# A sixth 8 KB gather buffer, idle tiles as further ones, and smaller scratch pools in a two-layer mixer with an expert layer

## The chip, the cores and the metric

The kernel runs on one core of a Trainium2 chip. The metric is the device time of one execution in microseconds (us). A core has five engines that each work through their own stream of instructions in order: TensorE (PE; PEld is its weight load), VectorE (DVE), ScalarE (ACT), GpSimd (POOL) and SyncE (SP). Sixteen DMA engines move data between HBM and the on-chip memory. In this kernel SP issues ordinary transfers (queue q1) and POOL issues the gathers by index (queue q0).

## What is computed

Two layers act on 256 latent tokens and 256 context tokens of width 1024, in float32. Each layer is a mixer (layer 0: a gated DeltaNet, "gdn", beside RWKV-7; layer 1: window attention beside a Hyena convolution) and behind it an expert layer, PEER. In layer 0 both streams go through both parts; in layer 1 only the latent stream does, while the attention reads the context's keys. The expert layer, cut to what matters:

```python
def peer(h, peer_wq, peer_k1, peer_k2, peer_u, peer_v):
    ...
        best, pos = lax.top_k(cand, PEER_TOPK)
        eid = jnp.take_along_axis(cid, pos, axis=-1)
        gate = jax.nn.softmax(best, axis=-1)
        u = jnp.take(peer_u, eid, axis=0)
        act = jax.nn.gelu(jnp.einsum('bthkd,btd->bthk', u, xb).astype(F32))
        vsel = jnp.take(peer_v, eid, axis=0)
        return jnp.einsum('bthk,bthkd->btd', (gate * act).astype(xb.dtype), vsel)
```

Every token has 8 heads with 16 experts each out of 16384, so 128 rows of u and 128 rows of v, each of 1024 numbers. Rows u and v of an expert lie side by side in HBM, 8 KB in all.

## The kernel before

Tokens are worked on in tiles of 128. `experts()` does one tile (or part of one): for each n of 128, POOL gathers the n-th expert's row for each of the 128 tokens (L1277) into a tile of the tag g8, 8 KB on each partition and 1 MB in all. VectorE multiplies its u half with the token and sums (L1280). ScalarE and VectorE make the gated activation from that (L1286 to L1289), ScalarE puts it on a diagonal, di (L1290), and TensorE multiplies di with the v half, 512 columns at a time, and adds into two banks of PSUM, pv (L1292). The profile shows two records for each of these two matmuls. The gathered buffer comes free when the second has read it.

There are 768 gathers: context tiles pc[0] (128) and pc[1] (64 first, 64 later, split at CUT), latent tiles pl[0] and pl[1], and in layer 1 p3[0] and p3[1]. At the end of a tile `experts()` takes a g8 tile for the residual and, in layer 1, another for the final norm. g8 also holds blocks of mod_w (1 MB each), from which `adaln` makes the modulation at the start.

Buffers: `Net.t(tag, shape)` takes a tile of a tag, and the dictionary BUFS says how many buffers a tag has (1 where it isn't named). A tile that finds none free waits until an older one's last reader is done. The tags that the change touches: g8; t2, s2 and sy, scratch tiles of the mixers (2 KB a partition for t2 and s2 at their widest); gx (one column, made in L1288) and gsum, small tiles of the expert layer and its preparation. s2 also holds the transposed probabilities PT of a pair of heads in `attention` (transposes L1524, copies L1526, matmuls L1530), while eight s2 tiles hold the output weights wo. h8 and qkT are single tiles: h8 is the layer's input in transposed form (two tiles long), and both hold query weights of PEER in layer 1 (`keep_wq`).

The order is not written out by hand. Python lays the steps down in program order, with generators that mix stages (`mix`, `some`, `rest`) and marks that hold a stage back (`issue_after`), and a scheduler simulates the program and puts each engine's instructions in the order in which they become ready there, expert steps filling in beside the mixers. The numbers of buffers enter that simulation, so they change the order on all engines. The stages in time: modulation and context mixer (0 to about 490 us), experts of the context beside the latent mixer (to about 1256), the latent tile's output projection and preparation of its experts (to about 1352), then experts beside the second layer's mixer and, to the end, alone.

The gathers' descriptors are written by POOL into a memory that `dynamic_dma_scratch_size` sizes, 4096 bytes before.

Of the kernel before, what the change touches and what calls it, by code (L numbers as in the profile page):

```python
# [20 lines left out]
D = 1024  # L21
# [7 lines left out]
def _lay(i):  # L29
# [83 lines left out]
    for n in ("b1", "b2", "freq"):  # L113
# [32 lines left out]
    return A  # L146


BUFS = dict(w=3, t2=9, t4=3, s2=10, AT=4, XT=2, N=2, sy=8, g8=5, ei=16, ef=2, best=2, pos=2, i16f=2, eid=2, pk=2, pf=2, gate=4, v16=2, i16=2, kTh=2, ftok=2,
            act=2, gz=3, gx=3, di=3, fnr=2, gsum=2, rT=2, nr=4, nr2=2, nr3=2, am=4, t2r=2, t2v=2, t2v2=2)  # L150
PBUFS = dict(gm=3, sc=3, pv=2)
CUT = 64

# [1 line left out]
class Net:  # L155
# [14 lines left out]
    def t(self, tag, shape, dt=F32):  # L170
        self.n += 1
        if tag in PBUFS:
            return self.psum[tag].tile(shape, dt, name=f"{tag}_{self.n}", tag=tag)
        return self.sb.tile(shape, dt, name=f"{tag}_{self.n}", tag=tag, bufs=BUFS.get(tag, 1))

# [1084 lines left out]
        nc.vector.reciprocal(gs, gs)  # L1260
        nc.vector.scalar_tensor_tensor(gate, gate, 0.5 / RT2PI, gs[:, :, None].to_broadcast([128, m, 16]), op0=ALU.mult, op1=ALU.mult)

    def experts(self, l, xin, cond, p, dst, fin=None, ns=range(128)):


        nc, A = self.nc, self.A
        h = p.h
        if h is None:
            h = self.t("h4", [128, D])
            nc.sync.dma_start(h, p.hd)  # L1270
        if p.act is None:
            p.act = self.t("act", [128, 128])
        act, gate = p.act, p.gate.rearrange("p h k -> p (h k)")
        pv = [self.t("pv", [128, 512]) for _ in range(2)]
        for n in ns:
            uv = self.t("g8", [128, 2 * D])
            nc.gpsimd.indirect_dma_start(out=uv, out_offset=None, in_=A[l + "peer_uv"],  # L1277
                                         in_offset=bass.IndirectOffsetOnAxis(ap=p.ei[n // 16][:, n % 16:n % 16 + 1], axis=0))
            x = act[:, n:n + 1]
            ins = nc.vector.scalar_tensor_tensor(uv[:, :D], uv[:, :D], RT2PI, h, op0=ALU.mult, op1=ALU.mult, accum_out=x)  # L1280
            if n == ns[0] + 8:
                self.mark = ins.ins
            with self.tc.high_priority():

                z, xg, di = self.t("gz", [128, 2]), self.t("gx", [128, 1]), self.t("di", [128, 128])
                nc.scalar.activation(z[:, 0:1], x, AF.Square, scale=math.sqrt(0.044715) / RT2PI)  # L1286
                nc.scalar.activation(z[:, 0:1], z[:, 0:1], AF.Tanh, scale=x, bias=x)  # L1287
                nc.vector.tensor_mul(xg, x, gate[:, n:n + 1])  # L1288
                nc.scalar.activation(z[:, 1:2], z[:, 0:1], AF.Identity, scale=xg, bias=xg)  # L1289
                nc.scalar.activation(di, self.ident, AF.Copy, scale=z[:, 1:2])  # L1290
                for hf in range(2):
                    nc.tensor.matmul(pv[hf], lhsT=di, rhs=uv[:, D + hf * 512:D + (hf + 1) * 512], start=n == ns[0], stop=n == ns[-1])  # L1292
            yield
        xr = self.t("g8", [128, 2, D])
        x1, rgt = xr[:, 0], xr[:, 1]
        nc.sync.dma_start(x1, xin)
        nc.sync.dma_start(rgt, self.mod[l][cond:cond + 1, 5 * D:6 * D].to_broadcast([128, D]))
        for hf in range(2):
            cs = slice(hf * 512, (hf + 1) * 512)
            nc.vector.tensor_mul(rgt[:, cs], pv[hf], rgt[:, cs])  # L1300
            nc.vector.tensor_add(x1[:, cs], x1[:, cs], rgt[:, cs])
        if fin:
            xf = self.t("g8", [128, 2, D])
            fn = xf[:, 0]
            nc.sync.dma_start(fn, A[fin].to_broadcast([128, D]))
            r = self.rstd(x1, "fn", xf[:, 1])
            nc.vector.scalar_tensor_tensor(x1, x1, r, fn, op0=ALU.mult, op1=ALU.mult)
        if ns[0] == 0 or "x2d1" in self.want:
            nc.sync.dma_start(dst, x1)
        self.xlast = x1  # L1310
# [350 lines left out]
    def whole(self, out):  # L1661
        nc, tc, A = self.nc, self.tc, self.A
        with ExitStack() as es:
# [5 lines left out]
            x1 = [self.d(f"x1d{c}", [T, D]) for c in range(2)]  # L1669
            x2 = [[self.d(f"x2d{c}{i}", [128, D]) for i in range(2)] for c in range(2)]  # L1670
            x3 = [self.d(f"x3d{i}", [128, D]) for i in range(2)]
            row = lambda a, i: a[i * 128:(i + 1) * 128]
            lat, ctx, odd = Stream(), Stream(), Stream()
            pc, pl, p3 = [], [], []
# [14 lines left out]
            def peer(*a, **k):  # L1689
                rest(self.experts(*a, **k))  # L1690
# [91 lines left out]
            some(g, 7)  # L1782
            peer("l0_", row(x1[1], 0), 1, pc[0], x2[1][0])
            peer("l0_", row(x1[1], 1), 1, pc[1], x2[1][1], ns=range(CUT))
            peer("l0_", row(x1[0], 0), 0, pl[0], x2[0][0])
            with tc.issue_after(self.mark):
                rest(g)
            peer("l0_", row(x1[0], 1), 0, pl[1], x2[0][1])
# [47 lines left out]
            for i in range(2):  # L1836
                self.dumprow("x3d", x3[i], i)
            self.dump("yT", odd.yT[0])
            peer("l1_", x3[1], 0, p3[1], row(out, 1), "fnorm")


class Stream:
# [19 lines left out]
```

## Time and profile before

| | |
|---|---|
| runs (us) | 3276.64, 3277.8, 3294.03; median 3277.8 |
| profiled execution (us) | 3273.96, its span 3272.2 |
| TensorE busy (us) | 2603.5 (80% of the span) |
| VectorE busy (us) | 1957.6 (60%) |
| ScalarE busy (us) | 1395.2 (43%) |
| GpSimd busy (us) | 987.4 (30%) |
| moved by DMA | 1020.52 MB, of which 805.36 by gathers |

The profile is of one execution. Busy shares are means over stages with different limits, so the table by stage below shows for each stretch how long each engine was busy and which share of the sixteen DMA engines' time was in use. A row of waits names the engine and the line that stood still, what ended the wait, and the total, the number and the longest of such waits. "<-PE pv L1292" behind a POOL instruction means that it waited for that matmul.

### The profile page before, as it was taken

What the parts mean: (1) busy time and instruction counts of PE and PEld (TensorE: products, weight loads), DVE (VectorE), ACT (ScalarE), POOL (GpSimd) and SP (SyncE); (2) the same over time, 40 slices, a digit from 0 to 9 for tenths busy, and PEclk for the clock granted to TensorE, in tenths of its full rate; (3) what the DMA queues carried; (4) which work ended last, traced back from release to release, by engine and by line L of the source; (5) the groups of instructions that cost most, each with busy time, mean ns of one, the idle gap of its engine ahead of it and who ended that gap; (6) DMA issues with size and microseconds to landing.
All of it is one profiled execution on the core that took longest, in us unless ns stands there. A gap on an engine that the chain in (4) does not pass through costs nothing.

```text
span 3272.2 us, 40186 instructions
## 1 busy us (share of the span) xinstructions
PE 2603.5 (80%) x12216; PEld 1447.9 (44%) x12216; DVE 1957.6 (60%) x5457; ACT 1395.2 (43%) x3953; POOL 987.4 (30%) x834
## 2 busy tenths in 40 slices
PE   6986867988888978696977777779967987767776
PEld 4765745754454535462422222235545543222222
DVE  2566546777956665579755555456547687554554
ACT  1431113465445545233554455544433544544554
POOL 0001202222322321124554344433202333434553
PEclk8886978999989989898999899999989999999999
DMA  9675549899889996587899999999947899999998
GB/s 324 214 230 143 191 143 343 318 343 335 322 290 333 339 319 206 214 305 260 298 379 385 355 387 384 378 371 347 363 153 284 306 338 352 377 369 379 384 390 324
DMA packets 296222, 1020.52 MB, mean 312 GB/s; under 512 B 64383, under 2 KB 167104, under 8 KB 197704
## 3 DMA queue, kind: packets, MB, share of 16 engines
q0 software_dynamic: 110592, 805.36, 64.5%
q1 hardware_dynamic: 185416, 212.60, 20.1%
q8 instruction: 99, 1.62, 0.2%
q14 instruction: 115, 0.94, 0.1%
HBM read 995.62 MB, written 22.25 MB: 311 GB/s over the span
## 4 chain that ended last, share of the span: by engine, by line
PE 32%; DMA 27%; issue 16%; DVE 14%; POOL 7%; ACT 3%; SPq 1%; POOLq 0%; DVEq 0%; ACTq 0%
DMA g<-in_l_peer_uv_dram,ei 17%; PE pv L1292 12%; POOL g L1277 6%; DVE g L1280 5%; PE gm L269 4%; PE gm L1142 3%; PE gm L1621 1%; DMA t<-in_l_mod_w_dram 1%; PE sc L269 1%; PE gm L277 1%; DMA w<-in_l_peer_wq_dram 1%; DMA qkT<-in_l_peer_wq_dram 1%; PE pv L356 1%; DMA g<-in_l_mod_w_dram 1%; DMA t<-l_mod 1%
## 5 line engine op out<-in xcount | busy, mean ns | idle before, releaser
L1292 PE MATMUL pv<-g,di 128*128 128x512 f32 x3072 | 1556.5, 635 | 421.7 <-ACT di L1290 420.4
L1277 POOL DMA_INDIRECT g<-in_l_peer_uv_dram,ei x768 | 927.6, 1208 | 1901.8 <-PE pv L1292 1109.7
L1292 PEld LDWEIGHTS pv<-g,di 128*128 128x128 f32 x3072 | 558.3, 198 | 1229.5 <-ACT di L1290 778.3
L1280 DVE SCALAR_TENSOR_TENSOR g<-g,h 128x1024 f32<-128x1024 f32 x384 | 469.8, 1224 | 309.3 <-DMA g<-in_l_peer_uv_dram,ei 304.2
L1286 ACT ACTIVATE gz<-act 128x1 f32<-128x1 f32 x768 | 154.8, 202 | 973.7 <-DVE g L1280 972.7
L1289 ACT ACTIVATE gz<-gz,gx 128x1 f32<-128x1 f32 x768 | 296.5, 386 | 68.6 <-DVE gx L1288 44.1
L1290 ACT ACTIVATE di<-c_ident,gz 128x128 f32<-128x128 f32 x768 | 307.6, 401 | 29.6 <-PE pv L1292 7.2
L1287 ACT ACTIVATE gz<-gz,act 128x1 f32<-128x1 f32 x768 | 296.2, 386 | 23.5
L1280 DVE SCALAR_TENSOR_TENSOR g<-g,vtok 128x1024 f32<-128x1024 f32 x128 | 157.0, 1227 | 155.3 <-DMA g<-in_l_peer_uv_dram,ei 153.3
L1280 DVE SCALAR_TENSOR_TENSOR g<-g,ktok 128x1024 f32<-128x1024 f32 x128 | 158.1, 1236 | 106.0 <-DMA g<-in_l_peer_uv_dram,ei 104.9
L1280 DVE SCALAR_TENSOR_TENSOR g<-g,yv 128x1024 f32<-128x1024 f32 x128 | 156.1, 1219 | 90.6 <-DMA g<-in_l_peer_uv_dram,ei 90.4
L269 PE MATMUL gm<-h,w 128*128 128x256 f32 x752 | 175.4, 380 | 2.1 <-DMA w<-in_l_w_in_dram 2.1
L269 PEld LDWEIGHTS gm<-h,w 128*128 128x128 f32 x752 | 141.3, 190 | 43.4 <-issue 24.4
L1288 DVE TENSOR_TENSOR gx<-act,gate 128x1 f32<-128x1 f32 x768 | 121.3, 158 | 52.0 <-ACT gz L1286 1.4
L1214 DVE MAX8 v<-t 128x8 f32<-128x128 f32 x64 | 15.5, 284 | 92.9 <-ACT t L1157 53.2
L1621 PE MATMUL gm<-og,w 128*128 128x128 f32 x384 | 52.4, 295 | 16.4 <-DMA w<-in_l_peer_wq_dram 16.4
L1621 PEld LDWEIGHTS gm<-og,w 128*128 128x128 f32 x384 | 51.0, 210 | 25.0 <-DMA w<-in_l_peer_wq_dram 17.0
L356 PE MATMUL pv<-t,scond 128*32 128x256 f32 x384 | 38.2, 493 | 28.8 <-DMA t<-in_l_mod_w_dram 28.7
L612 DVE TENSOR_TENSOR kTh<-dg 128x30 f32<-128x30 f32 (+14 forms) x120 | 40.2, 335 | 25.1 <-DMA dg<-dndg 22.8
L636 POOL MEMSET XT<- 32x512 f32 x4 | 2.1, 516 | 172.8 <-PE sc L269 172.7
L277 PE MATMUL gm<-w,h 128*128 128x256 f32 x192 | 47.9, 395 | 5.3 <-DMA w<-in_l_w_in_dram 5.3
L277 PEld LDWEIGHTS gm<-w,h 128*128 128x128 f32 x192 | 37.0, 197 | 17.9 <-issue 13.4
(686 smaller groups left out, 3127.9 us busy)
## 6 DMA issues: line engine op xcount, KB each, us to landing
w<-in_l_w_in_dram SPq DMA_DIRECT2D x70, 512.0 KB
g<-in_l_mod_w_dram SPq DMA_DIRECT2D x24, 1024.0 KB
t<-in_l_mod_w_dram SPq DMA_DIRECT2D x48, 512.0 KB
w<-in_l_peer_wq_dram SPq DMA_DIRECT2D x26, 512.0 KB
g<-in_l_peer_uv_dram,ei POOLq DMA_INDIRECT x768, 8.2
qkT<-in_l_peer_wq_dram SPq DMA_DIRECT2D x9, 1024.0 KB
XT<-in_l_peer_wq_dram SPq DMA_DIRECT2D x14, 512.0 KB
XT<-in_l_w_in_dram SPq DMA_DIRECT2D x10, 512.0 KB
```

The source lines that it names most:

```text
L269: self.nc.tensor.matmul(ps[:, m], lhsT=wt[q][:, k, m * 128:(m + 1) * 128], rhs=hk, start=q == 0 and m == 0 and k == 0, stop=q == 1 and m = ...
L277: self.nc.tensor.matmul(ps, lhsT=hk[:, i * 128:(i + 1) * 128], rhs=wt[k // 4][:, k % 4], start=k == 0, stop=k == KC - 1)
L1142: nc.tensor.matmul(pq[:, m], lhsT=w[1][k // 4][:, k % 4, m * 128:(m + 1) * 128], rhs=hT[i][:, k], start=k == 0, stop=k == KC - 1)
L1277: nc.gpsimd.indirect_dma_start(out=uv, out_offset=None, in_=A[l + "peer_uv"], in_offset=bass.IndirectOffsetOnAxis(ap=p.ei[n // 16][:, n % ...
L1280: ins = nc.vector.scalar_tensor_tensor(uv[:, :D], uv[:, :D], RT2PI, h, op0=ALU.mult, op1=ALU.mult, accum_out=x)
L1286: nc.scalar.activation(z[:, 0:1], x, AF.Square, scale=math.sqrt(0.044715) / RT2PI)
L1287: nc.scalar.activation(z[:, 0:1], z[:, 0:1], AF.Tanh, scale=x, bias=x)
L1288: nc.vector.tensor_mul(xg, x, gate[:, n:n + 1])
L1289: nc.scalar.activation(z[:, 1:2], z[:, 0:1], AF.Identity, scale=xg, bias=xg)
L1290: nc.scalar.activation(di, self.ident, AF.Copy, scale=z[:, 1:2])
L1292: nc.tensor.matmul(pv[hf], lhsT=di, rhs=uv[:, D + hf * 512:D + (hf + 1) * 512], start=n == ns[0], stop=n == ns[-1])
L1621: nc.tensor.matmul(pq[:, m], lhsT=wt[k // 4][:, k % 4, m * 128:(m + 1) * 128], rhs=hT[:, k], start=k == 0, stop=k == KC - 1)
```

## The change

It gives g8 six buffers instead of five, takes one buffer each from t2, s2, sy, gx and gsum, and halves the descriptor memory to 2048 bytes. `experts()` gets an argument `more`: behind each six tiles of g8 it takes one tile of each tag named there. For pl[0] that is h8 (seven buffers in a cycle), for the last tile, p3[1], h8 and qkT (eight). Both tags have one buffer and are between uses in those stretches. Line numbers behind L1276 are larger by one in the changed kernel.

```diff
-BUFS = dict(w=3, t2=9, t4=3, s2=10, AT=4, XT=2, N=2, sy=8, g8=5, ei=16, ef=2, best=2, pos=2, i16f=2, eid=2, pk=2, pf=2, gate=4, v16=2, i16=2, kTh=2, ftok=2,
-            act=2, gz=3, gx=3, di=3, fnr=2, gsum=2, rT=2, nr=4, nr2=2, nr3=2, am=4, t2r=2, t2v=2, t2v2=2)
+BUFS = dict(w=3, t2=8, t4=3, s2=9, AT=4, XT=2, N=2, sy=7, g8=6, ei=16, ef=2, best=2, pos=2, i16f=2, eid=2, pk=2, pf=2, gate=4, v16=2, i16=2, kTh=2, ftok=2,
+            act=2, gz=3, gx=2, di=3, fnr=2, gsum=1, rT=2, nr=4, nr2=2, nr3=2, am=4, t2r=2, t2v=2, t2v2=2)
...
-    def experts(self, l, xin, cond, p, dst, fin=None, ns=range(128)):
+    def experts(self, l, xin, cond, p, dst, fin=None, ns=range(128), more=()):
...
         for n in ns:
-            uv = self.t("g8", [128, 2 * D])
+            c = (n - ns[0]) % (BUFS["g8"] + len(more))
+            uv = self.t("g8" if c < BUFS["g8"] else more[c - BUFS["g8"]], [128, 2 * D])
...
-            peer("l0_", row(x1[0], 0), 0, pl[0], x2[0][0])
+            peer("l0_", row(x1[0], 0), 0, pl[0], x2[0][0], more=("h8",))
...
-            peer("l1_", x3[1], 0, p3[1], row(out, 1), "fnorm")
+            peer("l1_", x3[1], 0, p3[1], row(out, 1), "fnorm", more=("h8", "qkT"))
...
-    nc = bacc.Bacc("TRN2", target_bir_lowering=False, num_devices=1, dynamic_dma_scratch_size=4096)
+    nc = bacc.Bacc("TRN2", target_bir_lowering=False, num_devices=1, dynamic_dma_scratch_size=2048)
```

TensorE at the start of the latent gdn_scan (L684, L691, L707 are its steps, L1292 the matmuls of a context expert). Before:

```order
L684 MATMUL sc_1138_6997<-S0_67_288,qkT_912_5471 64x128 x8
L684 MATMUL sc_1139_6998<-S0_67_288,qkT_912_5471 64x128 x4
L1292 MATMUL pv_1892_10046<-g8_2094_10698,di_2097_10703 128x512
L1292 MATMUL pv_1893_10047<-g8_2094_10698,di_2097_10703 128x512
L684 MATMUL sc_1139_6998<-S0_67_288,qkT_912_5471 64x128 x4
L691 MATMUL sc_1142_7019<-s2_1140_7015,h8_1111_6737 64x64 x16
L1292 MATMUL pv_1892_10046<-g8_2098_10711,di_2101_10716 128x512
L1292 MATMUL pv_1893_10047<-g8_2098_10711,di_2101_10716 128x512
L707 MATMUL sc_1143_7046<-s2_1141_7016,s2_1137_6980 64x64 x8
L707 MATMUL sc_1144_7057<-s2_1141_7016,s2_1137_6980 64x64 x8
```

TensorE at the same place after the change:

```order
L684 MATMUL sc_1138_6997<-S0_67_288,qkT_912_5471 64x128 x8
L684 MATMUL sc_1139_6998<-S0_67_288,qkT_912_5471 64x128 x8
L691 MATMUL sc_1142_7019<-s2_1140_7015,h8_1111_6737 64x64 x16
L707 MATMUL sc_1143_7046<-s2_1141_7016,s2_1137_6980 64x64 x8
L707 MATMUL sc_1144_7057<-s2_1141_7016,s2_1137_6980 64x64 x8
```

Before, 178 gathers' matmuls stand ahead of the second L684 step and 14 of the context's 192 follow among the scan's steps; after, all 192 stand ahead of it.

POOL's gathers for the latent tile pl[0] (the seventh and its neighbours; the name in front is the tile that the gather fills). Before:

```order
L1277 DMA g8_2174_10956<-in_l0_peer_uv_dram,ei_1250_7723 128x2048
L1277 DMA g8_2178_10969<-in_l0_peer_uv_dram,ei_1250_7723 128x2048
L1277 DMA g8_2182_10982<-in_l0_peer_uv_dram,ei_1250_7723 128x2048
L1277 DMA g8_2186_10995<-in_l0_peer_uv_dram,ei_1250_7723 128x2048
L1277 DMA g8_2190_11008<-in_l0_peer_uv_dram,ei_1250_7723 128x2048
```

POOL's gathers for the same tile after the change:

```order
L1278 DMA g8_2174_10956<-in_l0_peer_uv_dram,ei_1250_7723 128x2048
L1278 DMA h8_2178_10969<-in_l0_peer_uv_dram,ei_1250_7723 128x2048
L1278 DMA g8_2182_10982<-in_l0_peer_uv_dram,ei_1250_7723 128x2048
L1278 DMA g8_2186_10995<-in_l0_peer_uv_dram,ei_1250_7723 128x2048
L1278 DMA g8_2190_11008<-in_l0_peer_uv_dram,ei_1250_7723 128x2048
```

The seventh gather of the tile, and each seventh from there on, goes into h8; the order of the gathers themselves is the same.

## Rows read from the trace of the kernel before

**Rows 1.** The page: DMA queue q0, chain by line, the gathers' group.

```profile
q0 software_dynamic: 110592, 805.36, 64.5%
...
DMA g<-in_l_peer_uv_dram,ei 17%; PE pv L1292 12%; POOL g L1277 6%; DVE g L1280 5%; PE gm L269 4%; PE gm L1142 3%; PE gm L1621 1%; DMA t<-in_l_mod_w_dram 1%; PE sc L269 1%; PE gm L277 1%; DMA w<-in_l_peer_wq_dram 1%; DMA qkT<-in_l_peer_wq_dram 1%; PE pv L356 1%; DMA g<-in_l_mod_w_dram 1%; DMA t<-l_mod 1%
...
L1277 POOL DMA_INDIRECT g<-in_l_peer_uv_dram,ei x768 | 927.6, 1208 | 1901.8 <-PE pv L1292 1109.7
```

**Rows 2.** Stretches: window, length, busy time by engine, clock, DMA share, GB/s.

```profile
490.00:1256.00 766.00, 666.70 (x3736) 404.14 (x3738) 528.66 (x1541) 393.18 (x1114) 214.38 (x202) 0.93 0.91 325
1256.00:1352.00 96.00, 62.99 (x460) 49.33 (x456) 45.85 (x155) 22.55 (x73) 0.46 (x2) 0.87 0.40 131
1352.00:1560.00 208.00, 158.22 (x706) 99.32 (x707) 162.17 (x610) 76.72 (x236) 67.09 (x52) 0.89 0.83 300
1560.00:1800.00 240.00, 194.22 (x421) 72.21 (x420) 141.55 (x292) 119.84 (x342) 120.01 (x89) 0.99 0.92 352
1800.00:2164.00 364.00, 263.57 (x538) 94.63 (x538) 185.57 (x413) 179.43 (x522) 160.23 (x128) 0.97 0.97 378
2164.00:2400.00 236.00, 212.03 (x640) 119.88 (x640) 127.60 (x283) 101.04 (x288) 63.38 (x60) 0.94 0.95 356
2400.00:2480.00 80.00, 61.24 (x384) 52.55 (x384) 43.91 (x165) 23.36 (x67) 4.69 (x5) 0.92 0.22 73
2480.00:2750.00 270.00, 224.83 (x920) 136.26 (x920) 204.75 (x699) 119.52 (x365) 78.93 (x72) 0.96 0.90 333
2750.00:3272.00 522.00, 376.36 (x734) 131.24 (x732) 267.30 (x589) 255.04 (x740) 236.87 (x179) 0.96 0.95 370
```

**Rows 3.** DMA of 1860 to 2140: GB/s in 40 slices, q0, issues to landing.

```profile
GB/s 426 373 410 397 375 399 421 342 412 344 398 386 341 424 391 364 417 351 410 400 351 377 357 425 360 413 370 386 403 348 404 312 424 399 375 380 425 323 419 373
...
q0 software_dynamic: 14792, 107.69, 98.0%
...
g<-in_l_peer_uv_dram,ei POOLq DMA_INDIRECT x102, 8.5
```

**Rows 4.** Two dips of the DMA share, columns as in Rows 2.

```profile
1464.00:1476.00 12.00, 10.46 (x52) 7.99 (x53) 4.76 (x27) 3.40 (x10) 0.94 (x1) 0.72 0.48 170
...
2684.00:2700.00 16.00, 13.51 (x50) 9.33 (x51) 8.13 (x31) 5.31 (x17) 3.67 (x3) 0.82 0.62 200
```

**Rows 5.** Waits of VectorE in 1352 to 1560: total, times, longest.

```profile
DVE g L1280 <- DMA g<-in_l_peer_uv_dram,ei: 18.8, 13, 3.7
```

**Rows 6.** The same in 1560 to 2400.

```profile
DVE g L1280 <- DMA g<-in_l_peer_uv_dram,ei: 311.8, 225, 8.4
```

**Rows 7.** The same in 2480 to 2750.

```profile
DVE g L1280 <- DMA g<-in_l_peer_uv_dram,ei: 24.6, 20, 3.1
```

**Rows 8.** The same in 490 to 1256.

```profile
DVE g L1280 <- DMA g<-in_l_peer_uv_dram,ei: 73.9, 48, 4.1
```

**Rows 9.** The stretch 1216 to 1256, columns as in Rows 2.

```profile
1216.00:1256.00 40.00, 38.37 (x474) 23.19 (x474) 27.36 (x59) 32.41 (x110) 11.84 (x11) 0.97 0.72 265
```

**Rows 10.** Groups by line in 1214 to 1256: count, busy and mean, idle before.

```profile
L1292 PE MATMUL pv<-g,di 128*128 128x512 f32 x44 | 22.8, 655 | 1.1 <-ACT di L1290 1.1
```

**Rows 11.** POOL's timeline: start, duration, instruction, idle before and its releaser.

```profile
1255.31 0.94 POOL L1277 DMA_INDIRECT g<-in_l_peer_uv_dram,ei  x1 [0.39 <-PE pv L1292]
...
1351.79 0.94 POOL L1277 DMA_INDIRECT g<-in_l_peer_uv_dram,ei  x1 [95.54 <-issue]
```

**Rows 12.** TensorE's timeline in the attention of latent tile 0.

```profile
2442.11 1.90 PE L1530 MATMUL gm<-S,s 128*128 128x64 f32 x16
```

**Rows 13.** ScalarE's timeline at the same place.

```profile
2440.20 1.07 ACT L1526 COPY s<-gm 128x512 f32<-128x512 f32 x2 [0.23 <-PE gm L1524]
```

**Rows 14.** SP's queue, loads of the context's rwkv_scan into s2 tiles.

```profile
291.08 0.32 SPq L882 DMA_DIRECT2D s<-kr  x1
294.28 0.32 SPq L883 DMA_DIRECT2D s<-bk  x1
```

**Rows 15.** TensorE's timeline, the first reader of these loads.

```profile
301.91 1.95 PE L892 MATMUL pv<-s,s 64*128 64x128 f32 x16
```

## The prediction

> **What bounds the kernel now.** I read the page first. TensorE is busy for four fifths of the span, which looks like a bound; but the queue of the gathers, q0, took 64.5% of the sixteen DMA engines' time for 805.36 MB, and the chain of waits gives gathers landing (17%) more of the span than the expert matmuls (12%) [rows 1]. The 768 gathers of L1277 waited 1109.7 us for "PE pv L1292", that is for a free g8 buffer, whose last reader is that matmul [rows 1].
>
> The table by stage then tells which resource is short where [rows 2]. From 490 us on the DMA engines are busy for 0.83 to 0.97 of each stretch that holds gathers, and for 0.40 and 0.22 of the two that hold nearly none. In 1860 to 2140, a stretch of gathers only, q0 alone moved 107.69 MB at 98.0% [rows 3]. One gather is 8192 bytes times 128 rows and 144 packets (110592 / 768), so its 14792 packets are 102.7 gathers in 280 us at that load, and 0.98 x 280 / 102.7 = **2.67 us of DMA for one gather**. No buffer gets a gather under that; the actual pitch there was 280 / 102.7 = 2.73. A sixth buffer can win only time in which the DMA engines stood idle.
>
> **Term 1: idle DMA that another buffer fills, from 1352 us on.** The idle share times the length of the stretches of [rows 2] from 1352 on, without 2400 to 2480, is 35 + 19 + 11 + 12 + 27 + 26 = 130 us. It comes in dips: a mixer step holds an in-order engine, the buffers in flight land, and no free one is left for the next issue. The DMA shares in slices of 4 us give 30 such dips; two of the larger ones stand in [rows 4]. An added buffer puts one more gather into a dip, so a dip pays back at most its idle time and at most 2.67 us for each added buffer: one in most tiles, two in pl[0] (1352 to about 1750), three in the last tile (about 2896 to 3256). So the dip of [rows 4] at 2684, with 16 x 0.38 = 6.1 us idle, pays 2.67, and the one at 1464, with 12 x 0.52 = 6.2, pays 5.3. Summed so by stretch of [rows 2]: 29.0, 12.9, 4.3, 8.3, 15.6 and 3.8 us. It also pays only if VectorE later stood waiting for a gather. That wait is 18.8 us in 1352 to 1560, 311.8 in 1560 to 2400 and 24.6 in 2480 to 2750 [rows 5 to 7]; it cuts only the first figure, to 18.8. The upper bound is 18.8 + 12.9 + 4.3 + 8.3 + 15.6 + 3.8 = 64 us. The lower is 0: the buffer after a long mixer step is freed by the same matmul, and expert n+6 may be held by the same TensorE, VectorE or ScalarE queue as n+5. I take the middle, **-32**, since no row prefers an end.
>
> **Term 2: the context experts in 490 to 1256.** Two things move. VectorE waited 73.9 us there for gathers [rows 8], and the DMA was idle for 0.09 x 766 = 69 us [rows 2], so the sixth buffer may help as above. And the order of TensorE changes: before, the latent gdn_scan (L684 and after) runs between the last 14 experts, which are all done ahead of it after the change (the fences on the change). In 1216 to 1256 TensorE was busy for 38.37 of 40 us, the DMA for 0.72 of it [rows 9], and the experts' matmuls were 22.8 us of it [rows 10]. So the scan alone would be some 23 us shorter, and 14 x 2.67 = 37 us of gathers must fit into the work ahead. If all of that fits into idle DMA, the stretch wins 23 and what the waits give besides, up to 60 in all; if nothing fits, it loses 37 - 23 = 14. Ahead of 1216 the idle DMA is 69 - 40 x 0.28 = 58 us, more than 37, but in small dips. I take **-10**, with ends of -60 and +14.
>
> The stretch without gathers behind it, 1255.31 to 1351.79 [rows 11], doesn't shrink: the output projection and the preparation of the latent tiles run alone there. All that the change adds is seven gathers instead of five at its end, counted in term 1.
>
> **Term 3: the pools that give way.** s2 from 10 to 9: while attention runs, the output weights (wo) hold eight, so one is left where two were for the pair of PT tiles. Before, both copies of a pair take 1.07 us, begun 0.23 after the transposes and ahead of 16 matmuls of 1.90 [rows 12, 13]. With one buffer it goes copy, eight matmuls, copy, eight matmuls: the second copy (1.07 / 2 = 0.54) and two more handovers of 0.23 come between the matmuls, 1.0 us a pair, and on the four pairs of tile 0, which lie in the stretch without gathers, **+4**. Ends: 0 if the second copy is hidden, +8 if tile 1's four pairs count too; these run beside the gathers, so I leave them out.
>
> t2, sy, gx, gsum and s2 elsewhere: I laid the buffers that the changed program assigns over the times of before. 47 tiles would find their buffer still in use. Nearly all have slack: the loads L882 and L883 are issued at 291.08 and 294.28, and their first reader runs at 301.91 [rows 14, 15]. What is left is about 2 us ahead of 490, and 8.7 for a t2 tile of peer_prep (L1237) near 795 us, beside gathers that hide it. **+2**, with ends of 0 and +11. Three of the 768 gx tiles would wait, 4.8 us in all, inside term 1's range. The early SP queue brings l0 mod_w loads forward and w_in loads back; the same bytes in another order, at nothing, with ends of -5 and +5.
>
> **Term 4: half of the descriptor memory.** The trace doesn't show how full it is. 4096 bytes served five gathers in flight without POOL being held: a gather instruction took 0.94 us both ahead of and behind the idle stretch [rows 11]. I take 0; the price if that is wrong is rival 3.
>
> The Trainium skill ("DMA: Bandwidth & Descriptors", section "The descriptor swizzle") says that a transfer of 1 MiB to 128 partitions needs nine write descriptors on each engine, and its "Terms" give 16 bytes for one. This case's trace agrees on the count: 144 packets for a gather are 16 x 9. By these figures 2048 bytes hold 2048 / 144 = 14 gathers (an estimate from that page), more than the eight in flight, so that the term would be 0.
>
> **The sum**, against the profiled execution's 3273.96: -32 - 10 + 4 + 2 = -36, so 3238. The median of the runs shown is 3277.8, 3.8 above the profiled run, so **3242**.
>
> **Rivals.** *1, nothing gained, 3270.* The sixth gather is held by what held the fifth: each engine is in order, a mixer step delays experts n to n+6 alike, and DMA is at its floor elsewhere. For it: at a share of 0.97 and 0.95 the stretches from 1800 to 2400 offer 23 us in all [rows 2]. Against it: VectorE's 311.8 us of waits for gathers [rows 6] are far more than the dips there would need. Terms 1 and 2 near 0, terms 3 and 4 stay: 3278 + 6 at the top, 3262 at the bottom.
>
> *2, slower through the order, about 3300.* Experts run ahead of mixer steps that the end depends on: 14 ahead of the gdn_scan, and about 20 at a later step of TensorE's order. If each such gather finds the DMA busy, it delays the mixer by 2.67 us: +14 in term 2, and as much again as the capped gain of term 1 isn't won. 3278 + 14 + 6 = 3298. It decides when the dips ahead of 1216 are too short for a whole gather. For it: DVE's wait in 490 to 1256 has 48 pieces of 4.1 us at most [rows 8], of which many are under 2.67. Against it: 58 us of idle DMA.
>
> *3, slower through the descriptor memory, about 3500.* If 4096 bytes were just enough for five gathers, 2048 carry 2.5. A gather takes 8.5 us from issue to landing in the pure stretch [rows 3], so the pitch would be 8.5 / 2.5 = 3.4 instead of 2.73: +0.67 on the 350 gathers or so of the pure stretches, +230. POOL's gathers would show it, at several us each. The two rows at 0.94 speak neither for nor against.
>
> *4, much faster, 3180.* The waits of 490 to 1256 also go (-60) and both bounds of term 1 are reached (-64), less 6 paid in pools: 3278 - 118 = 3160 at most; with half of the added part, 3180. In the same direction points a rate that rises with more gathers queued: single slices of the pure stretch reach 426 GB/s against a mean of 107.69 MB / 280 us = 385 [rows 3]. At 425 the 280 us would be 254, and the 350 gathers of the pure stretches would win some 87 us, to 3190. Against it: the queue was never empty at 98%.
>
> The Trainium skill (the same page, "Measured") has 341 GB/s for a transfer of 1 MB alone and 425 for one of 16 MB, which would mean that a deeper queue moves bytes faster. The trace's 385 with five in flight lies between, and no run here yet shows six.
>
> **How the numbers follow.** Forecast (3203 to 3261): 0.61. Nothing gained (3262 to 3284): 0.20. Slower through the order: 0.10. Descriptor memory: 0.04. Much faster: 0.05. The range runs from 3200 to 3288 and leaves out 0.18: rivals 3 and 4, and most of rival 2. A measurement of this kernel can tell about 0.5%, or 16 us, from no change. Faster by that (under 3261): 0.61 + 0.05 = 0.66. Within it (to 3294): 0.20 and a little of rival 2, 0.22. Slower: 0.12.
>
> **What would show it.** In the changed kernel's table by stage the DMA share of 1352 to 1800 and of the stretch around 2480 to 2750 rises to 0.9 or more (term 1), while the pitch of the pure stretches stays at 2.67 or above; below that, rival 4's rate is right. The first gather after the idle stretch is issued 5 to 30 us ahead of 1351.79 (term 2); at 1360 or later, rival 2. The copies of L1527 appear one by one between matmuls of L1531 (term 3). POOL's gathers stay at 0.94 us (term 4). If the dips keep their length with six buffers, rival 1 is right, and the sum fails at term 1.

## The result: 3148 us, 4% faster, and the profile after

The changed kernel takes 3148.06 us in the median of four runs (3140.3 to 3161.81) against 3277.22 before (3271.96 to 3294.03). The ratio is 0.9602, with a 95% interval of 0.9549 to 0.9655: 129 us less, where 36 were forecast, and below the stated range. The profiled execution is the slowest of the four, 3161.81 with a span of 3159.9, which is 112.3 less than the span before.

Lines behind L1276 are larger by one here: L1278 is the gather, L1281 VectorE's product, L1293 the expert matmul. First the page of the changed kernel: queue q0, the chain by line, and the gathers' group (they answer to [rows 1]).

```profile
q0 software_dynamic: 110592, 805.36, 64.6%
...
PE pv L1293 14%; POOL g L1278 13%; DMA g<-in_l_peer_uv_dram,ei 7%; PE gm L269 4%; DVE g L1281 4%; PE gm L1142 3%; PE gm L1622 2%; DMA t<-in_l_mod_w_dram 2%; DMA w<-in_l_w_in_dram 1%; PE sc L269 1%; DMA w<-in_l_peer_wq_dram 1%; DMA g<-in_l_mod_w_dram 1%; PE pv L356 1%; POOL h L1278 1%; DMA qkT<-in_l_peer_wq_dram 1%
...
L1278 POOL DMA_INDIRECT g<-in_l_peer_uv_dram,ei x718 | 975.2, 1358 | 1576.5 <-PE pv L1293 712.6
```

The same bytes crossed in 112 us less. Gathers landing fell from 17% of the chain to 7%, while POOL's own part in gathers rose from 6% to 13%. The wait for a free buffer fell from 1109.7 to 712.6 us; this is the wait of the 718 gathers into g, and the other 50 go into h8 and qkT.

Now the table by stage (window, length, busy time by engine, granted clock, DMA share, GB/s; the packets' recorded times overlap a little, so a share can pass 1), for the stretches that answer to [rows 2], the windows moved along with the stages:

```profile
486.00:1250.00 764.00, 663.03 (x3614) 403.45 (x3614) 530.01 (x1552) 386.59 (x1094) 230.54 (x202) 0.93 0.90 330
1250.00:1348.00 98.00, 62.78 (x576) 54.76 (x576) 44.00 (x147) 26.30 (x89) 0.00 (x0) 0.83 0.29 92
1348.00:1548.00 200.00, 156.73 (x710) 99.51 (x710) 153.88 (x583) 76.36 (x237) 61.38 (x55) 0.90 0.88 325
1548.00:1740.00 192.00, 172.10 (x378) 67.05 (x377) 135.81 (x292) 105.68 (x304) 111.82 (x78) 0.97 0.94 373
1740.00:2080.00 340.00, 264.92 (x551) 94.66 (x552) 189.24 (x422) 183.14 (x534) 219.64 (x131) 0.99 1.00 413
2080.00:2330.00 250.00, 232.15 (x710) 130.79 (x709) 144.70 (x332) 111.25 (x322) 72.47 (x66) 0.97 0.95 363
2398.00:2660.00 262.00, 214.81 (x879) 130.15 (x878) 189.16 (x635) 113.88 (x348) 87.96 (x76) 0.94 0.91 344
2660.00:3160.00 500.00, 379.59 (x814) 137.99 (x812) 289.07 (x689) 260.15 (x762) 292.42 (x180) 0.98 0.96 391
```

The line that the prediction didn't allow is the one from 1740 on: 131 gathers in 340 us, at 413 GB/s. Before, the stretch that held the same tile took 364 us for 128, at 378 GB/s and a share of 0.97 [rows 2]. The share had said "full"; the rate hadn't.

The DMA view of a stretch of gathers only, 1780 to 2060 (GB/s in 40 slices, q0's packets, MB and share, the gathers' count and median us to landing):

```profile
GB/s 430 423 421 395 420 417 420 420 424 419 423 417 427 420 421 417 424 420 422 420 421 423 421 421 420 422 417 403 408 424 419 425 420 422 412 421 411 406 420 405
...
q0 software_dynamic: 15865, 115.57, 99.7%
...
g<-in_l_peer_uv_dram,ei POOLq DMA_INDIRECT x111, 9.8
```

Before, the slices swung between 312 and 426 GB/s at 98.0% [rows 3], and the share of the engines' time in the same 40 slices didn't show it (a 9 is 90% or more):

```profile
DMA  9999999999999999999999999999999999999999
```

After, the slices lie near 420. So 426 wasn't a lucky slice but the engines' own pace, and the time of a packet shows it: 0.980 x 16 x 280 / 14792 = 0.297 us before, 0.997 x 16 x 280 / 15865 = 0.282 after, small packets included. In the trace's packet records the median packet of 8 KB takes 309 ns before and 312 after; but before, 5.8% of them took over 400 ns in this stretch and 6.4% in the last tile, after 0.4% and 0.6%. These long packets are counted as busy time.

Where the 112.3 us of the profiled spans went is read from POOL's timeline, at the first gather of the latent tiles, the first of layer 1 and the last. After:

```profile
1205.58 1.87 POOL L1278 DMA_INDIRECT g<-in_l_peer_uv_dram,ei  x1 [3.22 <-DVE yv L1021]
...
1348.16 0.94 POOL L1278 DMA_INDIRECT g<-in_l_peer_uv_dram,ei  x1 [140.71 <-issue]
...
2398.36 0.94 POOL L1278 DMA_INDIRECT g<-in_l_peer_uv_dram,ei  x1 [100.35 <-issue]
...
3126.42 1.95 POOL L1278 DMA_INDIRECT qkT<-in_l_peer_uv_dram,ei  x1 [0.54 <-PE pv L1293]
```

And the two of before that [rows 11] doesn't hold:

```profile
2472.48 0.94 POOL L1277 DMA_INDIRECT g<-in_l_peer_uv_dram,ei  x1 [89.80 <-issue]
...
3247.22 0.94 POOL L1277 DMA_INDIRECT g<-in_l_peer_uv_dram,ei  x1 [1.52 <-PE pv L1292]
```

| stretch | before | after | difference |
|---|---|---|---|
| start to the first latent gather | 1351.8 | 1348.2 | -3.6 |
| to the first gather of layer 1 | 1120.7 | 1050.2 | -70.5 |
| to the last gather | 774.7 | 728.1 | -46.7 |
| to the end | 25.0 | 33.5 | +8.5 |

Most of the last row is the price of a deeper queue: with eight buffers a gather of the last tile took 14.7 us in the median from issue to landing, where it took 8.5 with five.

### The profile page after: what moved, and what is told of

Read it like the earlier page. It is cut to its first block, busy times and chain, and to the rows that moved or that the text cites. A ratio compares the mean times of both kernels' runs of the same rounds, so it can differ in the third digit from the quotient of the medians.

```text
span 3159.9 us, 40234 instructions
## 1 busy us (share of the span) xinstructions
PE 2584.2 (82%) x12216; PEld 1452.8 (46%) x12216; DVE 1955.8 (62%) x5457; ACT 1384.4 (44%) x3947; POOL 1116.7 (35%) x834
## 4 chain that ended last, share of the span: by engine, by line
PE 38%; DMA 18%; POOL 14%; DVE 13%; issue 13%; ACT 3%; SPq 1%; POOLq 0%; DVEq 0%; ACTq 0%
PE pv L1293 14%; POOL g L1278 13%; DMA g<-in_l_peer_uv_dram,ei 7%; PE gm L269 4%; DVE g L1281 4%; PE gm L1142 3%; PE gm L1622 2%; DMA t<-in_l_mod_w_dram 2%; DMA w<-in_l_w_in_dram 1%; PE sc L269 1%; DMA w<-in_l_peer_wq_dram 1%; DMA g<-in_l_mod_w_dram 1%; PE pv L356 1%; POOL h L1278 1%; DMA qkT<-in_l_peer_wq_dram 1%
## 5 line engine op out<-in xcount | busy, mean ns | idle before, releaser
L1293 PE MATMUL pv<-g,di 128*128 128x512 f32 x2872 | 1427.6, 627 | 288.0 <-ACT di L1291 287.5
L1278 POOL DMA_INDIRECT g<-in_l_peer_uv_dram,ei x718 | 975.2, 1358 | 1576.5 <-PE pv L1293 712.6
L1293 PEld LDWEIGHTS pv<-g,di 128*128 128x128 f32 x2872 | 518.5, 195 | 1020.7 <-ACT di L1291 594.8
L1281 DVE SCALAR_TENSOR_TENSOR g<-g,h 128x1024 f32<-128x1024 f32 x352 | 429.6, 1221 | 179.2 <-DMA g<-in_l_peer_uv_dram,ei 178.5
L1281 DVE SCALAR_TENSOR_TENSOR g<-g,vtok 128x1024 f32<-128x1024 f32 x128 | 156.8, 1225 | 128.0 <-DMA g<-in_l_peer_uv_dram,ei 128.0
L1281 DVE SCALAR_TENSOR_TENSOR g<-g,yv 128x1024 f32<-128x1024 f32 x128 | 156.0, 1219 | 60.4 <-DMA g<-in_l_peer_uv_dram,ei 60.4
L1281 DVE SCALAR_TENSOR_TENSOR g<-g,ktok 128x1024 f32<-128x1024 f32 x110 | 134.0, 1219 | 54.1 <-DMA g<-in_l_peer_uv_dram,ei 52.5
L1293 PE MATMUL pv<-h,di 128*128 128x512 f32 x136 | 68.2, 625 | 17.9 <-ACT di L1291 17.9
L1278 POOL DMA_INDIRECT h<-in_l_peer_uv_dram,ei x34 | 53.8, 1581 | 47.3 <-PE pv L1293 21.5
```

## The experiments

Theory A, formed on the two traces, supposes that with five buffers the DMA engines ran out of queued gathers again and again for moments that the busy share doesn't show; what decides is how long a buffer is away from the queue, so a sixth buffer brings the pure stretches to the engines' own pace. Against it stood B (the smaller descriptor memory, or the tiles' new places, made packets faster) and C (five gathers can't be carried faster, whenever they come). Each diff is against the changed kernel, but for the four buffers and the two on buffers that come free earlier, which start from the kernel before; of the long line of BUFS only the part that changes is shown. Below, "pitch" is the time from one gather's issue to the next, as a mean over the pure stretches of the second latent tile and of the last tile.

### Smaller pools alone

```diff
-t2=8, t4=3, s2=9, AT=4, XT=2, N=2, sy=7, g8=6
+t2=8, t4=3, s2=9, AT=4, XT=2, N=2, sy=7, g8=5
...
-            peer("l0_", row(x1[0], 0), 0, pl[0], x2[0][0], more=("h8",))
+            peer("l0_", row(x1[0], 0), 0, pl[0], x2[0][0])
...
-            peer("l1_", x3[1], 0, p3[1], row(out, 1), "fnorm", more=("h8", "qkT"))
+            peer("l1_", x3[1], 0, p3[1], row(out, 1), "fnorm")
```

> The changed kernel with g8 back at five buffers and without the idle tiles: only the smaller pools and the halved descriptor memory are left of the change. Theory A (the sixth buffer keeps the DMA engines' queues from running empty; with five, some 7% of the 8 KB packets of the pure stretch took over 400 ns where the rest took 309): the rate of the pure gather stretches stays at 385 GB/s, the time is that of before plus the price of the pools, 3275 to 3295. Rival B (the smaller descriptor memory, or the new places of the tiles, make the packets faster): 410 GB/s and more in the pure stretches with five buffers too, and a time of 3200 or less.

3262.28 us, ratio 0.9986 (0.9954 to 1.0019): no difference from before, and not the 3275 to 3295 that was expected. Its table by stage, the two pure stretches:

```profile
1860.00:2100.00 240.00, 177.09 (x342) 62.31 (x340) 118.55 (x256) 117.97 (x343) 114.44 (x87) 0.95 0.97 374
2910.00:3190.00 280.00, 207.01 (x409) 71.54 (x409) 142.08 (x307) 140.51 (x408) 135.99 (x102) 0.98 0.98 382
```

B is out: with 2048 bytes and the new places the rate is the old one.

### Six buffers without the idle tiles

```diff
-            peer("l0_", row(x1[0], 0), 0, pl[0], x2[0][0], more=("h8",))
+            peer("l0_", row(x1[0], 0), 0, pl[0], x2[0][0])
...
-            peer("l1_", x3[1], 0, p3[1], row(out, 1), "fnorm", more=("h8", "qkT"))
+            peer("l1_", x3[1], 0, p3[1], row(out, 1), "fnorm")
```

> The changed kernel without the idle tiles h8 and qkT: six buffers everywhere. Theory A: 410 to 420 GB/s in all pure stretches, the last tile at 2.5 to 2.6 us a gather like the tile before; the time 3150 to 3175, since the idle tiles only help to fill the dips of the first latent tile. Rival (the idle tiles bring a good part): 3190 or more, and the last tile back at 2.7 us.

3139.19 us, ratio 0.961 (0.9566 to 0.9654), the same as the whole change within the intervals. The last tile has a pitch of 2.53 us, and its rate is that of the changed kernel with eight:

```profile
1835.00:2050.00 215.00, 170.14 (x344) 58.25 (x344) 119.62 (x258) 117.77 (x343) 157.93 (x86) 1.00 1.01 418
2820.00:3075.00 255.00, 201.33 (x408) 68.80 (x406) 141.55 (x306) 139.60 (x406) 179.12 (x102) 1.00 1.01 420
```

The time is below the expected 3150 to 3175. So given six buffers, h8 and qkT bring nothing that can be measured.

### The idle tiles without the sixth buffer

```diff
-t2=8, t4=3, s2=9, AT=4, XT=2, N=2, sy=7, g8=6
+t2=9, t4=3, s2=10, AT=4, XT=2, N=2, sy=8, g8=5
...
-            act=2, gz=3, gx=2, di=3, fnr=2, gsum=1,
+            act=2, gz=3, gx=3, di=3, fnr=2, gsum=2,
...
-dynamic_dma_scratch_size=2048
+dynamic_dma_scratch_size=4096
```

> The kernel before with the idle tiles alone: h8 as a sixth buffer for the first latent tile, h8 and qkT as a sixth and seventh for the last; all pools and the descriptor memory as before. Theory A: the last tile runs at 2.5 to 2.6 us a gather and about 415 GB/s, the tiles with five buffers stay at 2.73 and 385; time 3225 to 3255. Rival B (descriptor memory): the last tile stays at 2.7 us, time about 3270.

3226.28 us, ratio 0.9869 (0.9827 to 0.991). The two pure stretches of this one kernel differ as the buffers do, five in the first, seven in the second:

```profile
1865.00:2100.00 235.00, 171.70 (x344) 59.05 (x344) 119.93 (x259) 118.36 (x345) 120.06 (x87) 0.99 0.98 385
2910.00:3160.00 250.00, 198.27 (x403) 68.26 (x402) 137.25 (x296) 136.32 (x396) 182.62 (x102) 1.00 1.01 419
```

### Four buffers

```diff
-t2=9, t4=3, s2=10, AT=4, XT=2, N=2, sy=8, g8=5
+t2=9, t4=3, s2=10, AT=4, XT=2, N=2, sy=8, g8=4
```

> The kernel before with four g8 buffers. Theory A: a round of a buffer of 12.2 to 13.7 us (a gather lands a little sooner behind three others than behind four) over four buffers is 3.05 to 3.4 us a gather and 305 to 345 GB/s in the pure stretches, packets over 400 ns well above 6%; time 3380 to 3550. Rival (the DMA was at its floor of 2.67 us with five buffers, as the prediction had it): 2.75 us, 380 GB/s, time 3290 to 3320 through the dips alone.

3467.32 us, ratio 1.058 (1.0528 to 1.0633), pitch 2.98 and 3.04 us, and 10% of the 8 KB packets over 400 ns:

```profile
1970.00:2220.00 250.00, 173.75 (x340) 59.99 (x340) 118.96 (x258) 118.28 (x344) 89.69 (x86) 0.97 0.95 356
3090.00:3390.00 300.00, 214.02 (x404) 73.70 (x403) 138.89 (x300) 137.77 (x400) 105.77 (x100) 0.94 0.93 347
```

A floor of 2.67 us with five buffers near it would have meant little loss here. It is no fixed cost either: worked out as the prediction did, from the share and the pitch, a gather's DMA time is 0.95 x 2.95 = 2.8 us in the first of these stretches (1 MB at 356 GB/s is 2.95 us), where it was 2.67 with five buffers and 1.01 x 2.51 = 2.53 with six. The pitch is a little below A's 3.05 to 3.4: a gather landed 6.4 us after its issue in the median, where it took 8.5 with five.

### A buffer that comes free earlier, first try

```diff
-                for hf in range(2):
+                for hf in range(2 if n in (ns[0], ns[-1]) else 1):
```

> The kernel before, five buffers, with the second of the two expert matmuls (v columns 512 to 1023) left out for all experts but the first and the last of each call; the second half of the expert sum isn't computed. A buffer comes free some 1.2 us earlier (two of four records of 592 ns). Theory A: what counts is how long a buffer is away from the DMA queue (5 x 2.73 = 13.7 us a round before); 12.5 / 5 = 2.5 us is the DMA's own pace at 309 ns a packet, so the pure stretches come to 2.5 to 2.6 us a gather and 405 GB/s or more, and packets over 400 ns fall from 6% to 3% or less, with five buffers. Rival C (the packets' pace goes with the number of gathers queued, and five can't do better): 2.7 us and 385 GB/s as before.

One run, 3227.97 us, pitch 2.77 and 2.74: at first sight C. But the edit took work from TensorE, and its clock fell. The table by stage and the group by line of 1850 to 2070 in this kernel:

```profile
1850.00:2070.00 220.00, 152.26 (x162) 37.43 (x162) 111.72 (x241) 110.49 (x321) 108.66 (x81) 0.60 0.98 383
```

```profile
L1292 PE MATMUL pv<-g,di 128*128 128x512 f32 x162 | 152.8, 1043 | 67.8 <-ACT di L1290 67.8
```

The two records that were left took 1043 ns each, where four of 624 ns stood in the same kind of stretch before: 2.09 us against 2.50, so the buffer came free 0.4 us earlier, not 1.2. By A's sum that alone would have given (13.7 - 0.4) / 5 = 2.66 us, which wasn't reached; a gather took 9.0 us to land in this stretch, where it took 8.5. One run, with the clock changed, doesn't tell A from C.

### A buffer that comes free earlier, with TensorE's work kept

```diff
-                    nc.tensor.matmul(pv[hf], lhsT=di, rhs=uv[:, D + hf * 512:D + (hf + 1) * 512], start=n == ns[0], stop=n == ns[-1])
+                    nc.tensor.matmul(pv[hf], lhsT=di, rhs=h[:, 512:] if hf else uv[:, D:D + 512], start=n == ns[0], stop=n == ns[-1])
```

> The kernel before, five buffers, with the second expert matmul of each gather reading the token tile in place of the gathered v columns 512 to 1023; the second half of the expert sum is another sum then, TensorE's work is the same. A buffer comes free after the first two of the four records, some 1.2 us earlier, and the clock stays as before (in e5 it fell to 0.60 in the pure stretch and the two records that were left took 1043 ns each). Theory A: 13.7 - 1.2 = 12.5 us a round, 2.5 to 2.6 us a gather, 400 GB/s or more, packets over 400 ns at 4% or less, time 3160 to 3220. Rival C (five gathers can't be carried faster, whenever they come): 385 GB/s, 2.74 us, 6%, time 3255 or more.

3167.14 us, ratio 0.9661 (0.9629 to 0.9692), pitch 2.54 and 2.52, packets over 400 ns 0.8%. With five buffers, the old pools and 4096 bytes:

```profile
1845.00:2060.00 215.00, 170.02 (x344) 58.26 (x344) 119.77 (x258) 117.78 (x343) 80.05 (x87) 1.00 1.01 418
2850.00:3100.00 250.00, 197.03 (x398) 67.46 (x399) 138.67 (x298) 136.45 (x397) 94.16 (x100) 1.00 1.01 417
```

C is out: with no buffer added, five gathers were carried at 418 GB/s, and 109 us are there, where the whole change brought 129. In the kernel before, a gather goes out some 0.3 us behind the end of all four records; the first three lines are of that kernel, the other three of this one, where it goes out 0.3 us behind the end of two ("<-DVE gx" is only the event that came last by the profile):

```profile
1905.09 1.98 PE L1292 MATMUL pv<-g,di 128*128 128x512 f32 x4 [0.53 <-ACT di L1290]
1907.29 1.23 DVE L1280 SCALAR_TENSOR_TENSOR g<-g,vtok 128x1024 f32<-128x1024 f32 x1 [0.92 <-DMA g<-in_l_peer_uv_dram,ei]
1907.35 1.98 POOL L1277 DMA_INDIRECT g<-in_l_peer_uv_dram,ei  x1 [1.58 <-PE pv L1292]
...
1904.75 1.23 DVE L1280 SCALAR_TENSOR_TENSOR g<-g,vtok 128x1024 f32<-128x1024 f32 x1 [0.99 <-DMA g<-in_l_peer_uv_dram,ei]
1905.06 1.13 PE L1292 MATMUL pv<-g,di 128*128 128x512 f32 x2 [0.50 <-ACT di L1290]
1906.46 0.94 POOL L1277 DMA_INDIRECT g<-in_l_peer_uv_dram,ei  x1 [1.54 <-DVE gx L1288]
```

The lines show a second thing that shortened the round. Before, 41 of the 102 gathers in 1860 to 2140 took 1.9 us in place of 0.94, all of them begun while VectorE's product L1280 ran; here all 87 of the first stretch took 0.94. The run doesn't part the two. The hold by VectorE alone doesn't set the rate: with six buffers 79 of the 85 or so gathers were held so, at 418 GB/s. What is shown is that the time a buffer is away sets the rate; that an engine's own queue ran empty in the long packets is argued, since the records don't name the engine of a packet.

### The descriptor memory: 512, 1024 and 4096 bytes

Six buffers without the idle tiles, as above, and:

```diff
-dynamic_dma_scratch_size=2048
+dynamic_dma_scratch_size=512
```

> Six buffers without the idle tiles (as e2), descriptor memory 512 bytes instead of 2048. If the memory's size bounds the gathers in flight, and six need 6 x 144 = 864 bytes (an estimate from the Trainium skill, page DMA: Bandwidth & Descriptors, nine descriptors an engine at 16 bytes), three and a half stay in flight: POOL's gathers take several us each, and the time goes to 3300 or more. If it doesn't, time and rate are those of e2, 3139 and 418 GB/s.

3249.68 us, ratio 0.992 (0.9889 to 0.9952), 110 us more than with 2048. The rate falls to what five buffers gave:

```profile
1885.00:2115.00 230.00, 171.71 (x342) 59.07 (x340) 118.43 (x256) 118.09 (x343) 139.61 (x86) 0.99 0.99 390
2910.00:3190.00 280.00, 206.58 (x396) 71.76 (x396) 137.72 (x298) 136.23 (x396) 162.36 (x99) 0.95 0.97 372
```

POOL's timeline shows the hold not as instructions of several us but as idle time ahead of them that no engine ended ("issue"; 29 times in the first stretch, 36.4 us in all):

```profile
1955.80 1.63 POOL L1278 DMA_INDIRECT g<-in_l_peer_uv_dram,ei  x1 [1.32 <-issue]
1958.58 1.64 POOL L1278 DMA_INDIRECT g<-in_l_peer_uv_dram,ei  x1 [1.14 <-issue]
```

So the prediction's third rival exists, below 1024 bytes, but the loss is smaller than the 3300 or more that was expected. The next two set its place: 1024 bytes (with s2 at ten and t2 at seven), and 4096 (with t2 at seven and s2 at nine, so that it fits).

```diff
-t2=8, t4=3, s2=9,
+t2=7, t4=3, s2=10,
...
-dynamic_dma_scratch_size=2048
+dynamic_dma_scratch_size=1024
```

> As e7 (six buffers, s2 ten, t2 seven) with 1024 bytes of descriptor memory. At 512 bytes POOL's gathers were held after idle time that no other engine ended, and the pure stretches fell to 381 GB/s. If six gathers need 864 bytes (an estimate from the Trainium skill, page DMA: Bandwidth & Descriptors), 1024 carry them: 418 GB/s and 3130. If part of the memory can't be used, the rate falls between 385 and 418 and the time lies at 3150 to 3240.

3141.16 us, ratio 0.9588 (0.9558 to 0.9618), 420 GB/s in both pure stretches.

```diff
-t2=8, t4=3, s2=9,
+t2=7, t4=3, s2=9,
...
-dynamic_dma_scratch_size=2048
+dynamic_dma_scratch_size=4096
```

> Six buffers without the idle tiles, t2 at seven, s2 at nine, descriptor memory back at 4096 bytes. If halving it costs nothing, the pure stretches stay at 418 GB/s and the time is that of e2, 3130 to 3150. If 2048 held gathers back somewhere, it is 3120 or less, with the gain in the stretches of gathers.

3147.52 us, ratio 0.9607 (0.9582 to 0.9632), 419 GB/s. Neither end moves the rate: halving the memory was free, and a quarter of it would have done for six.

The Trainium skill's figure ("DMA: Bandwidth & Descriptors", "The descriptor swizzle": nine write descriptors an engine for such a transfer, at the 16 bytes of its "Terms") gives 864 bytes for six gathers, an estimate; that 1024 carried them and 512 didn't agrees with it. By the same figures 512 bytes would hold three and a half gathers, and the rate was that of five buffers, well above that of four; so the runs don't show how many bytes a gather holds, or for how long.

### s2 back at ten

```diff
-t2=8, t4=3, s2=9,
+t2=7, t4=3, s2=10,
```

> Six buffers without the idle tiles (as e2), with s2 back at ten and t2 at seven. The four head pairs of the first latent tile's attention take 21 us again, as before, instead of 29: -8 us against e2 if t2 gives nothing away, so about 3131. If a seventh t2 tile less costs as much, 3139 or more.

3129.64 us, ratio 0.9545 (0.9513 to 0.9576), against 0.961 (0.9566 to 0.9654) for the same kernel with s2 at nine and t2 at eight: the medians differ by the 9.6 us that were looked for, with intervals that overlap. The four head pairs of the first latent tile took 28.8 us from the first transpose to the last PT matmul in the changed kernel, and take 20.7 here, as before. TensorE's timeline of the changed kernel:

```profile
2353.18 1.00 PE L1531 MATMUL gm<-S,s 128*128 128x64 f32 x8
2354.91 1.10 PE L1531 MATMUL gm<-S,s 128*128 128x64 f32 x8 [0.73 <-ACT s L1527]
...
2359.17 1.00 PE L1531 MATMUL gm<-S,s 128*128 128x64 f32 x8
2360.90 1.10 PE L1531 MATMUL gm<-S,s 128*128 128x64 f32 x8 [0.73 <-ACT s L1527]
```

and of this one:

```profile
2351.08 1.89 PE L1531 MATMUL gm<-S,s 128*128 128x64 f32 x16
...
2356.13 1.90 PE L1531 MATMUL gm<-S,s 128*128 128x64 f32 x16
```

With one buffer the sixteen matmuls break into eight and eight, with a wait for the second copy between. This is the fastest version that was run, by its median; against the whole change (0.9549 to 0.9655) the interval doesn't part it.

### More of the context's experts early: CUT at 96 and 80

```diff
-CUT = 64
+CUT = 96
```

> The changed kernel with CUT at 96 instead of 64: 32 more of the second context tile's gathers are made early, where the DMA engines are idle for some two thirds of 1206 to 1348 once the 192 early gathers are done, and 32 fewer run beside the second layer's mixer. If the early stretch has room, the latent tile starts at about 1348 as now and the 32 gathers save up to 32 x 2.5 = 80 us later: 3080 to 3130. Rival: the in-order engines delay the latent mixer by as much as they win, first latent gather at 1380 or later, 3140 to 3180.

3152.23 us, ratio 0.9638 (0.9599 to 0.9677): not the 3080 to 3130 that was expected, but the rival's range, and the first latent gather came at 1394.9, 47 us later than in the changed kernel, as the rival had it. Still, 32 gathers more were done by then (between 1215 and 1325), and counted by number the gathers from there to the end of layer 0 ran 31 to 92 us ahead of the changed kernel's, the last of them 58. But the first gather of layer 1 came at 2393.55, 5 us ahead:

```profile
2130.00:2390.00 260.00, 223.95 (x866) 148.49 (x865) 125.63 (x313) 83.86 (x236) 37.48 (x32) 0.93 0.62 224
```

The DMA engines are at 0.62 there and TensorE is busy for 224 of 260 us: the gathers were done by 2239, and the second layer's mixer, attention and preparation were waited for.

```diff
-t2=8, t4=3, s2=9,
+t2=7, t4=3, s2=10,
...
-CUT = 64
+CUT = 80
```

> As e7 with CUT at 80: sixteen more gathers of the second context tile early. With 96 the later gathers ran some 40 us ahead up to the third expert tile and lost it again ahead of the second layer's attention, so the mixer was late there, not the gathers. If that holds, 3125 to 3145, no different from e7; if 64 was too small and 96 too large, 3110 or less.

3136.75 us, ratio 0.9549 (0.9503 to 0.9595): no different from the same kernel with CUT at 64.

## Why the prediction was wrong

**The floor under a gather, the step that failed.** The first part took 0.98 x 280 / 102.7 = 2.67 us as DMA time that no buffer can get a gather under. The busy share behind it counted the packets that took over 400 ns, some 6% of those of 8 KB. The engines' own pace is 128 x 0.31 / 16 = 2.48 us, and the changed kernel's pure stretch runs at 280 / 111 = 2.52. The trace before had shown it: slices of up to 426 GB/s beside a mean of 385 at an even share [rows 3] mean that the share isn't the rate. The prediction quoted the 426, called it a rate that rises with more gathers queued, and argued against it "the queue was never empty at 98%". That sentence was wrong. The fourth rival, at 3180 and a chance of 0.05, was nearest, and the measured time is below its lower end of 3160 too.

**Term 1, sized at -32 with an upper bound of 64.** From the first latent gather on, the table of the result has -70.5 - 46.7 + 8.5 = -108.7, with some 8 us of term 3 in it, so about -117. An estimate: 2.73 - 2.52 = 0.21 us on the 128 + 179 gathers of the stretches 1800 to 2164 and 2750 to 3272 [rows 2] are 64 us, of which (2.67 - 2.52) x 307 = 46 lie below the floor and were excluded by it. The other 50 or so lie beside the mixer, and no run parts them into dips that were filled and packets that got shorter there. The sign from 1348 on was right: the DMA share rose from 0.83 to 0.88 and from 0.92 to 0.94. A pitch below 2.67 was the prediction's own sign that rival 4's rate is right, and it came out so.

**Term 2, -10 with ends of -60 and +14.** It came to -3.6. The context's gathers were all issued by 1205.58, 50 us earlier than before [rows 11], so the 14 experts ahead of the gdn_scan did find room, and rival 2 didn't decide. But the latent mixer didn't become faster by it: the stretch without gathers grew from 96 to 142 us. The term asked whether gathers fit, and not whether anything waited for them. The size of -3.6 says little: these are single executions, and the same gather came at 1326.83 with the smaller pools alone, at five buffers, and at 1334.92 with six buffers without the idle tiles.

**Term 3, +4 for attention with ends of 0 and 8, +2 for the rest.** Attention measured 28.8 - 20.7 = +8.1. The mechanism and its rows were right, and at the full clock so was the size: from the third pair's transposes to the fourth's it is 5.98 us in the changed kernel and 5.05 with s2 at ten, 0.9 a pair. Most of the other half of the 8.1 goes with TensorE's clock, which the term didn't count. The table by stage of the changed kernel, a stretch at the lower level of 1.2 GHz for the most part and one at 2.4, and then the whole stretch with s2 at ten, where the clock never fell:

```profile
2348.00:2355.00 7.00, 6.07 (x26) 5.35 (x26) 0.21 (x2) 1.44 (x3) 0.00 (x0) 0.66 0.00 0
2355.00:2362.00 7.00, 5.89 (x41) 5.27 (x41) 0.29 (x1) 1.44 (x3) 0.00 (x0) 1.00 0.00 0
...
2342.40:2363.10 20.70, 18.40 (x128) 16.37 (x127) 5.99 (x19) 10.31 (x29) 0.00 (x0) 1.00 0.01 1
```

Just ahead of the first of two falls TensorE had waited 1.48 us for a second copy. In the time of the whole kernel the price doesn't show: with the smaller pools alone attention took 27.4 us and the time didn't rise (0.9986, at most some 6 us by its interval), and no run says what gave it back.

**Term 4, 0.** Right, and shown: 1024, 2048 and 4096 bytes give 420, 418 and 419 GB/s. The row that spoke for it, 0.94 us for a gather, was the wrong sign to look at, and the page had 1.21 in the mean already [rows 1]. POOL's gathers take 1.84 us in the mean with six buffers and 0.94 where five come free earlier, at the same 418 GB/s, and the real hold at 512 bytes shows as idle time ahead of the instruction.

The Trainium skill ("DMA: Bandwidth & Descriptors", "Measured") has 341 GB/s for 1 MB alone and 425 for 16 MB. The runs with several gathers of 1 MB queued lie between the two: 347 to 356 GB/s with four buffers, 374 to 385 with five, 418 to 420 with six, and 419 to 421 with seven and eight.

## What to carry to other kernels

A DMA share near 1 doesn't say that the engines are at their pace: compare GB/s with the best slices, and the mean packet with the median one. Where transfers pass through a ring of buffers, multiply pitch by buffers to get a buffer's round, and compare the pitch with the packets' own pace; until the two met, both a further buffer and one returned earlier paid here, and beyond it seven and eight buffers brought no more than six. Before costing a stretch that gets faster, ask what waits for its end: with the gathers done early, 100 and 142 us without gathers were left in which only the mixer counted.

## What the runs showed of the hardware that was not expected

- Half of the expert matmuls left out made TensorE slower: it was busy for 152 of 220 us with 162 matmuls, its granted clock was 0.60 in the mean, so mostly the lower of its two levels (1.2 GHz), and a record took 1043 ns where it took 624 with twice the matmuls. An experiment that takes work from TensorE has to look at the clock first.
- Long packets count as busy: 8 KB packets over 400 ns were 10% with four buffers, 6% with five and under 1% with six, at shares of 0.93 to 1.01.
- POOL's gather instruction took 0.94 us or about twice that, and every long one began while VectorE's product ran: in 1860 to 2140 of the kernel before 41 of 102, each ending 0.81 us behind the product's end. Of the 61 short ones 7 began inside a product too. With six buffers 79 of some 85 were long, at the full rate.
- With 512 bytes of descriptor memory, six buffers did what five did (372 to 390 GB/s); with 1024 they ran at 420.
